# The first block's mixing in another order: plain transposes of x, squares of queries ahead of further weights, scores ahead of eight convolution taps on TensorE

## The chip, the cores and the metric

The kernel runs on one core of a Trainium2 chip. The metric is the device time of one execution in microseconds; lower is better. The core's engines are TensorE (PE, its weight loads PEld), VectorE (DVE), ScalarE (ACT), GpSimd (POOL) and SyncE (SP), which issues the loads of the large weights.

## What is computed

The input x has 256 rows (time steps) of 1024 channels. A first block mixes the rows and applies a mixture of 16 experts; a second block with another mixer and 32 experts follows. All is float32. The change lies in the first block's mixing, which in the reference reads, cut to what matters:

```python
def first_block(x, ...):
    h = rms_norm(x, attn_norm_g)
    z = h @ w_in
    a_val, a_gate, p_in, q, k, v = jnp.split(z, splits, axis=-1)
    u = a_val * sigmoid(a_gate)                       # 256 channels
    y_conv = silu(layer_norm(causal_conv31(u) + conv_b)) @ w_pw + b_pw
    y_pool = pool_mixer(p_in, pool_w, pool_scale)     # 256 channels, windows of 2, 4, 8, 16
    q = rms_norm(q.reshape(..., 4, 2, 64), q_norm_g)  # k likewise
    lam = exp(sum(lq1 * lk1)) - exp(sum(lq2 * lk2)) + lam_init
    # per head: softmax(first half) - lam * softmax(second half), times v
    y_attn = rms_norm(diff_attention(q, k, v, lam, slopes), sub_norm_g) * (1 - lam_init)
    x = x + concatenate([y_conv, y_pool, y_attn]) @ w_out
    hf = rms_norm(x, ffn_norm_g)
    return x + hier_moe(hf, ...)
```

The rms norm of x multiplies each row by a number r of its own and each channel by a gain. Since r is one number per row it may be applied before the product with `w_in` or after it.

## The kernel before, in words

x is held as two tiles of 128 rows (`xr`). TensorE needs the channels on the partitions, so x is turned into eight pieces of 128 channels by 256 rows. `rms_r` computes r, `diagonal` writes it on two diagonal matrices `rdg` (L432), and `transpose_split` multiplies x by them, so that turning and scaling are one product (`ptr`). Each piece is scaled by the gain (`colG`) on its way out of PSUM and split in a high part (`h1h`, ScalarE, L415) and a remainder (`h1l`, VectorE).

The weights are loaded in pieces: `piece` loads two halves by SP, and splits each in `hi` (ScalarE, L235) and `lo` (VectorE, L236). A product with `w_in` is then three products of TensorE: hi by h1h, lo by h1h, hi by h1l. The jobs of list `J1` hold such a piece each and run in the order in which they were added: queries, keys (`row`, result `pr`), gate, value (`ch`, result `pg`, channels on the partitions), `vv`, pool, six jobs of the modulation vector that the second block needs (`pada`: 16 products each; ScalarE's `adap`, `pac`), two of `w_out`, three more of modulation. `ahead` issues loads and splits of coming jobs; in the order that results they stand on ScalarE's and VectorE's queues among the other work.

The other work of the stage is written as generators, and `weave` takes steps of jobs and of generators alternately, at a rate (`RATE1`). The program's scheduler then orders each engine's instructions. `qk_chain` computes lambda from four small loads (`lamv`), the squares (`qsq`) and their sums (`qs`), a reciprocal root, the normalised queries and keys, and turns them (`pqt`). `conv_chain` runs the 31 taps of the convolution: the first with bias by a VectorE operation (L758), 20 by VectorE's multiply-and-add (L771, 40 instructions since there are two groups of channels), ten by ScalarE multiplications (L751) that GpSimd adds up (L768), and one addition (L777) brings the two sums together. Then follow the mean and variance by TensorE (`pmean`, `pvar`), the norm, silu (L798) and the product `ppw`. `attn_head` computes scores (`psc`), adds the distance term (L844), maxima, exponentials (ScalarE L851), the difference of the two softmaxes (L857, L858), turns it (`pat`), and multiplies it by `vv` (`po`). `attn_end` normalises the four heads' outputs and turns them (`poT`). `pool_chain` forms the windows' sums on VectorE and its product is `ppl`.

After that `ctx_prep` turns the second block's context (`ptr` of `xc`), the product with `w_out` is added to x, x is turned (`ptm`) for the router's logits (`plg`), and the router places the rows (`ppos`, `Dd`) for the first gather `pgx` of the experts.

Tiles of 8 KB come from a pool of 19 slots, PSUM from two pools of four banks (`mm` for jobs, `aux` for the rest).

Of the kernel before, what the change touches and what calls it, by code (L numbers as in the profile page):

```python
# [11 lines left out]
F32R = mybir.dt.float32r  # L12
# [10 lines left out]
KD = 8  # L23
# [7 lines left out]
ADA1 = 6  # L31
ADAR = 3
RATE1 = 1.3
RATE2 = 1.3
# [7 lines left out]
YA = 3  # L42
NPOOL = 10
TACT = 1
FILL = 2
# [77 lines left out]
def _body(es, tc, I, cst_d, msk_d, out_d, tap, stop):  # L123
# [9 lines left out]
    def U(name, shape, dt=F32):  # L133
        return gp.tile([128] + shape, dt, tag="g8", name=name)
# [520 lines left out]
    J1.row(w_in, 1792, h1f, (0, 128), lambda j, p: A.activation(t1["vv"][:, j, :], p, AF.Copy))  # L655
    J1.ch(w_in, 512, h1f, 256, lambda c, p: A.activation(t1["ppad"][:, c, 16:272], p[:, :256], AF.Copy))
    for b in range(ADA1):
# [58 lines left out]
    def qk_chain():  # L716
        lp = W("lamp", [2, 64])
        lv4 = lamv.rearrange("p (a b) d -> p a b d", b=2)
        V.tensor_tensor(lp, lv4[:, :, 0, :], lv4[:, :, 1, :], op=ALU.mult)
        ls = S("lams", [2], bufs=1)  # L720
        V.tensor_reduce(ls, lp, op=ALU.add, axis=AX.X)
        A.activation(ls, ls, AF.Exp)
        V.tensor_tensor(lam, ls[:, 0:1], ls[:, 1:2], op=ALU.subtract)
        V.tensor_scalar(lam, lam, lam_init, None, op0=ALU.add)
# [8 lines left out]
        V.tensor_tensor(qkv, qkv, qr.unsqueeze(2).to_broadcast([128, 32, 64]), op=ALU.mult)  # L733
        yield
# [14 lines left out]
    def TE(o, i, w):  # L749
        if TACT:  # L750
            A.activation(o, i, AF.Copy, scale=w)  # L751
        else:
            G.tensor_scalar(o, i, w, None, op0=ALU.mult)

    def conv_chain():

        for c in range(2):
            V.tensor_scalar(acc[:, c, :], upad[:, c, 0:256], colA[:, oCW + c:oCW + c + 1],  # L758
                            colA[:, oCB + c:oCB + c + 1], op0=ALU.mult, op1=ALU.add)

        last = 31 - NPOOL
        for j in range(last, 31):
            t = W("tap", [2, 256])
            for c in range(2):
                w = colA[:, oCW + 2 * j + c:oCW + 2 * j + c + 1]
                TE(sg1[:, c, :] if j == last else t[:, c, :], upad[:, c, j:j + 256], w)
            if j > last:
                G.tensor_tensor(sg1, sg1, t, op=ALU.add)  # L768
        for j in range(1, last):
            for c in range(2):  # L770
# [147 lines left out]
    left = weave(J1.run(ADA1), [att, chain(cvc, pool_chain())], RATE1)  # L918
    drain(both(*left))
# [1102 lines left out]
```

## Time and profile before

| | us |
|---|---|
| median of 3 runs | 1324.03 (1322.96 to 1325.92) |
| the profiled execution | 1325.26 |
| its span, first to last instruction | 1323.4 |
| TensorE busy | 1248.6 (94%) |
| VectorE busy | 662.1 (50%) |
| ScalarE busy | 424.9 (32%) |
| GpSimd busy | 38.5 (3%) |

The mean granted TensorE clock is 0.986. Sums are made against the profiled execution, which lies 1.2 us above the median. Shares of busy time over the whole span say little here, because the change lies in the first 170 us and the rest is another program; the rows of the section below are cut by stage.

### The profile page before, as it was taken

Reading aid. Unit: us, or ns where it says so; the run is one execution under the profiler, and the core shown is the slowest. Engines: PE = TensorE matmul, PEld = TensorE weight load, DVE = VectorE, ACT = ScalarE, POOL = GpSimd, SP = SyncE. Lnnn points to the kernel's source line nnn. Section 1 sums busy time; section 2 is a strip of 40 time slices with the busy share of each in tenths; the row PEclk is TensorE's granted clock in tenths of the full one; section 3 lists DMA queues with packets and bytes.
Section 4 is the critical chain, followed back from the end, with each engine's and each line's share of the span. In section 5 each row is a group of like instructions: output and inputs, shape, how many; then the busy total and the mean of one; then the engine's idle time right before and its main releaser. Section 6 shows DMA issues by size and latency. Waiting matters only on the chain. (4 is left out here: it accounts for less than half of the span.)

```text
span 1323.4 us, 19929 instructions
## 1 busy us (share of the span) xinstructions
PE 1248.6 (94%) x8098; PEld 852.8 (64%) x8098; DVE 662.1 (50%) x1444; ACT 424.9 (32%) x728; POOL 38.5 (3%) x50
## 2 busy tenths in 40 slices
PE   6988999999999999999999999899999998999895
PEld 5844566666788998898989889734435454444432
DVE  6895641125569987876574866632212222121222
ACT  5734322224334565544434443311111111010111
POOL 4110100000000000000000000100000000000000
PEclk9989899999999999999999999899999999999998
DMA  8798799983533241352525676799999999999993
GB/s 265 254 330 316 228 356 361 393 348 116 151 91 95 65 114 51 102 158 65 160 69 183 205 261 263 287 372 421 422 421 422 421 421 421 421 422 421 422 421 159
DMA packets 124355, 359.79 MB, mean 272 GB/s; under 512 B 15272, under 2 KB 64593, under 8 KB 97632
## 3 DMA queue, kind: packets, MB, share of 16 engines
q1 hardware_dynamic: 114224, 355.49, 70.6%
q10 hardware_dynamic: 9024, 2.24, 0.8%
q8 instruction: 67, 1.10, 0.3%
q0 software_dynamic: 1008, 0.70, 0.2%
q14 instruction: 32, 0.26, 0.1%
HBM read 357.35 MB, written 1.05 MB: 271 GB/s over the span
## 5 line engine op out<-in xcount | busy, mean ns | idle before, releaser
L156 PE MATMUL pg<-hT,hi 128*128 128x256 f32 (+1 forms) x1024 | 232.6, 321 | 1.5 <-DVE Qg L1363 1.5
L156 PE MATMUL pgu<-w,XT 128*64 128x256 f32 (+1 forms) x1088 | 185.9, 481 | 10.6 <-DMA w<-in_w_up_dram 10.6
L156 PEld LDWEIGHTS pg<-hT,hi 128*128 128x128 f32 x1024 | 167.2, 188 | 16.4 <-DVE Qg L1363 1.7
L236 DVE TENSOR_TENSOR lo<-w,hi 128x1024 fp32r<-128x1024 f32 x122 | 146.0, 1218 | 44.6 <-ACT hi L235 16.6
L156 PE MATMUL pdn<-w,actT 128*64 128x512 f32 x656 | 153.3, 597 | 15.6 <-ACT actT L1178 15.6
L156 PE MATMUL pg<-hT,lo 128*128 128x256 f32 (+1 forms) x512 | 162.4, 318 | 0.0
L235 ACT ACTIVATE hi<-w 128x1024 fp32r<-128x1024 f32 x122 | 125.1, 1053 | 95.5 <-PE pr L156 32.3
L156 PEld LDWEIGHTS pgu<-w,XT 128*64 128x64 f32 x1088 | 87.7, 137 | 102.2 <-issue 61.2
L156 PE MATMUL pgg<-w,XT 128*64 128x512 f32 x512 | 117.1, 596 | 1.1 <-DMA w<-in_w_gate_dram 1.1
L156 PEld LDWEIGHTS pdn<-w,actT 128*64 128x64 f32 x656 | 56.8, 136 | 94.8 <-issue 70.8
L156 PEld LDWEIGHTS pg<-hT,lo 128*128 128x128 f32 x512 | 96.2, 188 | 7.3 <-issue 0.4
L156 PE MATMUL pr<-hi,hT 128*128 128x256 f32 (+1 forms) x384 | 88.9, 321 | 0.6 <-PEq L1272 0.6
L156 PEld LDWEIGHTS pgg<-w,XT 128*64 128x64 f32 x512 | 37.0, 137 | 70.5 <-issue 63.9
L1167 DVE SCALAR_TENSOR_TENSOR act<-sgm,ws,pgu 128x512 f32<-128x512 f32 (+1 forms) x25 | 24.4, 977 | 101.7 <-PE pgu L156 101.7
L1193 DVE TENSOR_TENSOR Pg<-pdn,g 128x512 f32<-128x512 f32 x32 | 22.0, 689 | 99.4 <-PE pdn L156 99.4
L1159 DVE TENSOR_TENSOR sgm<-sgm,pgg 128x512 f32<-128x512 f32 x16 | 11.0, 688 | 116.9 <-ACT sgm L1158 116.8
L156 PEld LDWEIGHTS pr<-hi,hT 128*128 128x128 f32 x384 | 64.1, 188 | 7.2 <-issue 1.0
L1158 ACT ACTIVATE sgm<-pgg 128x512 f32<-128x512 f32 x16 | 9.6, 597 | 176.6 <-PE pgg L156 176.6
L1197 ACT ACTIVATE Ph<-Pg 128x512 fp32r<-128x512 f32 x32 | 20.2, 630 | 134.1 <-DVE Pg L1193 134.1
L156 PE MATMUL pr<-lo,hT 128*128 128x256 f32 (+1 forms) x192 | 61.8, 322 | 0.0
L156 PE MATMUL pgx<-Dd,xnh 128*128 128x256 f32 (+1 forms) x208 | 49.5, 283 | 0.1
L156 PE MATMUL pgx<-Dd,xnl 128*128 128x256 f32 (+1 forms) x208 | 49.3, 282 | 0.0
(520 smaller groups left out, 1928.4 us busy)
## 6 DMA issues: line engine op xcount, KB each, us to landing
w<-in_w_gate_dram SPq DMA_DIRECT2D x82, 1024.0 KB, 19.8
w<-in_w_up_dram SPq DMA_DIRECT2D x82, 1024.0 KB, 19.7
w<-in_w_down_dram SPq DMA_DIRECT2D x80, 1024.0 KB, 19.8
w<-in_w_in_dram SPq DMA_DIRECT2D x98, 512.0 KB, 4.6
w<-in_w_ada_dram SPq DMA_DIRECT2D x24, 1024.0 KB, 6.7
w<-in_w_out_dram SPq DMA_DIRECT2D x4, 1024.0 KB, 5.5
w<-in_w_branch_b_dram SPq DMA_DIRECT2D x8, 512.0 KB, 4.1
w<-in_w_branch_a_dram SPq DMA_DIRECT2D x8, 512.0 KB, 4.6
```

Source lines behind the costliest of these rows:

```text
L156: t2["mm"] = PE.matmul(out, lhsT, rhs, start=start, stop=stop, skip_group_check=True)
L235: t2["hi"] = A.activation(hi[:, ks], t, AF.Copy)
L236: t2["lo"] = V.tensor_tensor(lo[:, ks], t, hi[:, ks].bitcast(F32), op=ALU.subtract)
L1158: A.activation(sg, outs[0], AF.Sigmoid)
L1159: V.tensor_tensor(sg, sg, outs[0], op=ALU.mult)
L1167: V.scalar_tensor_tensor(act.rearrange("p (f c) -> p c f", f=NF), sg.rearrange("p (c f) -> p c f", f=NF), wcol, o.rearrange("p (c f) -> p ...
L1193: V.tensor_tensor(qg, q, gain[:, n, :], op=ALU.mult)
L1197: A.activation(ph, q, AF.Copy)
```

## The change

- x is turned by 16 plain transposes with the identity, before r is known. r is applied after the products: as ScalarE's scale on queries, keys and `vv` (rows on the partitions), and for gate, value and pool, where rows lie along the free dimension, by VectorE multiplications with a tile `rrow` that holds r in every partition. `rrow` comes from a product of ones with the diagonals (`prw`).
- In `qk_chain` the squares and their sums stand first, ahead of the parameters' transposes (`param_cols`) and of the splits of further weights; lambda comes after the turns of queries and keys.
- Eight taps (the last ones, 23 to 30) run on TensorE: ScalarE writes 16 diagonal matrices of 128 by 128 (`cdg`), and 16 products of 128 by 256 sum up in PSUM (`pcv`). VectorE does taps 0 to 22 (44 multiply-and-adds in place of 40). ScalarE's and GpSimd's taps go.
- Value and gate no longer share the weave with the convolution's start: `vv` comes after the query norm, and the convolution weaves with the attention and all remaining jobs. `RATE1` goes from 1.3 to 1.7, and the pool's generator waits until its input exists.

```diff
-RATE1 = 1.3
+RATE1 = 1.7
...
-NPOOL = 10
-TACT = 1
+NPE = 8
...
-               lambda j, p, qi=qi: A.activation(t1["qk"][:, 2 * qi + j, :], p, AF.Copy))
-    J1.ch(w_in, 256, h1f, 256, lambda c, p: A.activation(t1["sg1"][:, c, :], p[:, :256], AF.Sigmoid))
+               lambda j, p, qi=qi: A.activation(t1["qk"][:, 2 * qi + j, :], p, AF.Copy, scale=rx[:, j:j + 1]))
+
+    def ev_gate(c, p):
+        sg = t1["sg1"][:, c, :]
+        V.tensor_tensor(sg, p[:, :256], t1["rrow"], op=ALU.mult)
+        A.activation(sg, sg, AF.Sigmoid)
+        V.tensor_tensor(sg, sg, t1["rrow"], op=ALU.mult)
+
+    J1.ch(w_in, 256, h1f, 256, ev_gate)
...
-    J1.ch(w_in, 512, h1f, 256, lambda c, p: A.activation(t1["ppad"][:, c, 16:272], p[:, :256], AF.Copy))
+    J1.row(w_in, 1792, h1f, (0, 128), lambda j, p: A.activation(t1["vv"][:, j, :], p, AF.Copy, scale=rx[:, j:j + 1]))
+    J1.ch(w_in, 512, h1f, 256,
+          lambda c, p: t1.__setitem__("pp", V.tensor_tensor(t1["ppad"][:, c, 16:272], p[:, :256], t1["rrow"],
+                                                            op=ALU.mult)))
...
+    for kk in range(4):
+        p = ax_ps("ptr", (2, 256))
+        for i in range(2):
+            for j in range(2):
+                PE.transpose(p[:, j, 128 * i:128 * i + 128],
+                             xr[i][:, 128 * (2 * kk + j):128 * (2 * kk + j) + 128], ident)
+        for j in range(2):
+            k = 2 * kk + j
+            split_evac(h1[0][:, k, :], h1[1][:, k, :], p[:, j, :], colG[:, k:k + 1])
+        if kk == 1:
+            J1.ahead(1)
...
-    transpose_split(xr, rx, h1[0], h1[1], 0, colG, dg=rd)
+    t1["rrow"] = W("rrow", [256])
...
-    param_cols()
+    prw = ax_ps("prw", (256,))
+    for i in range(2):
+        mm(prw[:, 128 * i:128 * i + 128], ones, rd[:, i], True, True)
+    V.tensor_copy(t1["rrow"], prw)
...
+    def conv_taps():
+
+        dg = [U("cdg", [2, 8, 128]) for _ in range((NPE + 7) // 8)]
+        t1["cdg"] = lambda c, i: dg[i // 8][:, c, i % 8, :]
+        for i in range(NPE):
+            for c in range(2):
+                o = oCW + 2 * (31 - NPE + i) + c
+                A.activation(t1["cdg"](c, i), ident, AF.Copy, scale=colA[:, o:o + 1])
...
+        pcv = ax_ps("pcv", (2, 256))
+        for c in range(2):
+            for i in range(NPE):
+                j = 31 - NPE + i
+                mm(pcv[:, c, :], t1["cdg"](c, i), upad[:, c, j:j + 256], i == 0, i == NPE - 1)
...
-        if NPOOL:
-            V.tensor_tensor(acc, acc, sg1, op=ALU.add)
+        V.tensor_tensor(acc, acc, pcv, op=ALU.add)
...
-    weave(J1.run(2), [qk_chain()], 1.0)
+    qkc = qk_chain()
+    next(qkc)
+    param_cols()
+    with after(t2["qsq"]), after(t2["qkn"]):
+        J1.ahead(5)
     b1 = U("b1", [4, 512])
     vv = t1["vv"] = b1[:, 0:2, :]
     t1["osb"] = b1[:, 2:4, :]
-    cvc = conv_chain()
-    left = weave(J1.run(1), [cvc], 1.0)
     ppad = t1["ppad"] = U("ppad", [6, 288])
     V.memset(ppad[:, 0:2, 0:16], 0.0)
-    drain(J1.run(1))
+    drain(J1.run(2))
+    drain(qkc)
+    conv_taps()
     t1["ex"] = [U("ex", [2, 2, 512]) for _ in range(2)]
+    cvc = conv_chain()
     att = chain(both(*[attn_head(h) for h in range(4)]), attn_end())
-    left = weave(J1.run(ADA1), [att, chain(cvc, pool_chain())], RATE1)
+    left = weave(J1.run(2 + ADA1), [att, chain(cvc, pool_chain())], RATE1)
```

How the instructions are moved shows in the order of the engines' queues at three places. The lines of the changed kernel differ by up to some thirty from those of the kernel before.

The first place is ScalarE from the evacuation of the first keys (`qk<-pr`) to the squares (`qsq`); `cb` is the tile of constants, into which the weights of `conv_pw` and the pool are loaded as well, `lamv` holds the four vectors of lambda. Before:

```order
L651 ACTIVATE qk<-pr 128x512
L235 ACTIVATE hi<-w 128x1024
L701 DMA cb_367<-shape_consts 128x896
L706 DMA cb_367<-in_conv_pw_w_dram 128x2x256
L710 DMA cb_367<-in_pool_w_dram 64x64 x4
L235 ACTIVATE hi<-w 128x1024 x3
L651 ACTIVATE qk<-pr 128x512
L235 ACTIVATE hi<-w 128x1024
L651 ACTIVATE qk<-pr 128x512
L728 ACTIVATE qsq<-qk 128x2048
```

and in the changed kernel:

```order
L650 ACTIVATE qk<-pr,rry 128x512
L722 DMA cb_359<-shape_consts 128x896
L727 DMA cb_359<-in_conv_pw_w_dram 128x2x256
L650 ACTIVATE qk<-pr,rry 128x512
L731 DMA cb_359<-in_pool_w_dram 64x64 x4
L734 DMA lamv<-in_lambda_q_dram 128x64
L734 DMA lamv<-in_lambda_k_dram 128x64
L734 DMA lamv<-in_lambda_q_dram 128x64
L734 DMA lamv<-in_lambda_k_dram 128x64
L741 ACTIVATE qsq<-qk 128x2048
```

The loads of `lamv`, which stood far ahead among the first evacuations of x, now stand between the loads of `cb` and the squares.

The second place is VectorE around the sums of squares (`qs`); `lamp` is the product of lambda's vectors, `qry`, `qrh` and `qrt` belong to the reciprocal root, and `cv` holds the convolution's input, gate and sum. Before:

```order
L1509 TENSOR_TENSOR lbe<-colB,lbm 128x32
L730 TENSOR_REDUCE qs<-qsq 128x32
L596 TENSOR_TENSOR scp<-colC,sgc 128x8x2
L731 TENSOR_SCALAR qs<-qs 128x32
L377 TENSOR_SCALAR qry<-qs 128x32
```

and in the changed kernel:

```order
L1535 TENSOR_TENSOR lbe<-colB,lbm 128x32
L654 TENSOR_TENSOR cv<-pg,rrow 128x256
L763 TENSOR_TENSOR lamp<-lamv 128x128
L743 TENSOR_REDUCE qs<-qsq 128x32
L595 TENSOR_TENSOR scp<-colC,sgc 128x8x2
L654 TENSOR_TENSOR cv<-pg,rrow 128x256
L744 TENSOR_SCALAR qs<-qs 128x32
L656 TENSOR_TENSOR cv<-cv,rrow 128x256
L376 TENSOR_SCALAR qry<-qs 128x32
```

`lamp`, which needs all four loads, and the gate's multiplications by `rrow` have moved to the front of and between the steps of the reciprocal root.

The third place is TensorE from the convolution's last product `ppw` to the second head's output `po` and what follows it. Before:

```order
L156 MATMUL ppw<-cv,cb_367 128x256 x4
L156 MATMUL ppl<-dd,cb_367 128x256 x2
L156 MATMUL pada<-w,scp 32x512 x4
L863 MATMUL pat<-cst,ex 128x128 x3
L617 MATMUL pac<-cst,adap 128x128 x4
L156 MATMUL po<-b_569,aT 128x128 x3
L863 MATMUL pat<-cst,ex 128x128 x3
L156 MATMUL po<-b_569,aT 128x128 x3
L863 MATMUL pat<-cst,ex 128x128 x3
L156 MATMUL pr<-w,mix 128x512
```

and in the changed kernel:

```order
L155 MATMUL ppw<-cv,cb_359 128x256 x4
L155 MATMUL ppl<-dd,cb_359 128x256 x2
L884 MATMUL pat<-cst,ex 128x128 x3
L155 MATMUL pada<-w,scp 32x512
L155 MATMUL po<-b_426,aT 128x128 x3
L155 MATMUL pada<-w,scp 32x512 x3
L884 MATMUL pat<-cst,ex 128x128 x3
L616 MATMUL pac<-cst,adap 128x128 x4
L155 MATMUL po<-b_426,aT 128x128 x3
L884 MATMUL pat<-cst,ex 128x128 x3
L155 MATMUL pada<-w,scp 32x512
L155 MATMUL po<-b_426,aT 128x128 x3
```

Products of modulation (`pada`) have moved in behind `ppw` where pieces of `w_out` (`pr`) followed; ahead of `poT` six of those pieces are left where there were nine.

## Rows read from the trace of the kernel before

**Rows 1.** Busy time by stage: stretch, length, then busy us (instructions) of each engine, granted clock, DMA.

```profile
17.23:39.93 22.70, 22.70 (x100) 17.85 (x99) 15.69 (x24) 13.21 (x18) 1.75 (x4) 1.00 0.85 282
49.46:52.65 3.19, 0.00 (x0) 0.03 (x1) 3.12 (x8) 0.93 (x2) 0.00 (x0) 1.00 0.33 127
45.39:106.78 61.39, 49.14 (x316) 32.44 (x315) 59.00 (x149) 33.69 (x79) 11.39 (x9) 0.94 0.77 281
84.90:91.80 6.90, 5.08 (x21) 2.37 (x20) 6.56 (x29) 4.68 (x20) 0.00 (x0) 0.51 0.99 364
106.50:148.82 42.32, 41.08 (x166) 23.27 (x167) 18.94 (x63) 15.56 (x35) 0.00 (x0) 1.00 0.74 273
106.78:110.80 4.02, 4.02 (x23) 2.36 (x22) 3.92 (x15) 3.07 (x8) 0.00 (x0) 1.00 0.23 49
173.00:316.00 143.00, 137.70 (x996) 85.38 (x995) 37.06 (x81) 35.77 (x75) 0.00 (x0) 1.00 0.83 326
```

**Rows 2.** Timeline of TensorE, opening and context: start, us, instructions, idle time before and its releaser.

```profile
6.64 0.27 PE L212 MATMUL pcol<-cst,stage 8*128 8x8 f32 x1 [6.64 <-DMA stage<-in_attn_norm_g_dram]
10.95 6.55 PE L156 MATMUL ptr<-rdg,xr 128*128 128x128 f32 x32 [4.04 <-DVE rdg L432]
17.26 0.48 PE L156 MATMUL pr<-hi,h1h 128*128 128x512 f32 x1
...
130.48 3.73 PE L156 MATMUL ptr<-rdg,xc 128*128 128x128 f32 x32
```

**Rows 3.** Timeline of ScalarE up to the squares.

```profile
9.49 1.06 ACT L235 ACTIVATE hi<-w 128x1024 fp32r<-128x1024 f32 x1 [3.12 <-DMA w<-in_w_in_dram]
...
28.49 0.58 ACT L651 ACTIVATE qk<-pr 128x512 f32<-128x512 f32 x1
...
32.88 0.45 ACTq L706 DMA_DIRECT2D cb<-in_conv_pw_w_dram  x1
...
43.44 1.92 ACT L728 ACTIVATE qsq<-qk 128x2048 f32<-128x2048 f32 x1
```

**Rows 4.** Loads: of tile lamv, from issue to landing; of conv_pw, KB and us to landing.

```profile
DMA to landing us min/median/max: 4.1/4.4/6.2
...
cb<-in_conv_pw_w_dram ACTq DMA_DIRECT2D x1, 256.0 KB, 6.4
```

**Rows 5.** Timeline of VectorE from the squares to the router, and of GpSimd.

```profile
45.39 2.29 DVE L730 TENSOR_REDUCE qs<-qsq 128x32 f32<-128x2048 f32 x1 [0.24 <-ACT qsq L728]
...
55.81 2.35 DVE L236 TENSOR_TENSOR lo<-w,hi 128x1024 fp32r<-128x1024 f32 x2
58.08 0.42 DVE L654 TENSOR_TENSOR cv<-pg,cv 128x256 f32<-128x256 f32 x1
...
59.13 14.88 DVE L771 SCALAR_TENSOR_TENSOR cv<-cv,colA 128x256 f32<-128x256 f32 x16
...
73.97 4.80 DVE L771 SCALAR_TENSOR_TENSOR cv<-cv,colA 128x256 f32<-128x256 f32 x12
...
168.63 0.76 DVE L1089 TENSOR_TENSOR Dd<-cst,pe 128x256 fp32r<-128x256 f32 x2
...
59.72 12.02 POOL L768 TENSOR_TENSOR cv<-cv,tap 128x512 f32<-128x512 f32 x9 [39.93 <-ACT tap L751]
```

**Rows 6.** Timeline of TensorE from the queries' turns to the router.

```profile
52.65 1.94 PE L744 MATMUL pqt<-cst,qk 128*128 128x128 f32 x16 [3.19 <-DVE qk L733]
...
84.59 2.11 PE L156 MATMUL psc<-qkT 64*128 64x128 f32 x8 [4.07 <-DVE ex L844]
...
106.50 1.99 PE L156 MATMUL ppw<-cv,cb 128*128 128x256 f32 x8 [1.05 <-DVE cv L798]
...
111.07 0.66 PE L617 MATMUL pac<-cst,adap 128*128 128x128 f32 x4 [0.24 <-ACT adap L614]
...
124.43 0.74 PE L893 MATMUL poT<-cst,b 128*128 128x128 f32 x5 [0.37 <-DVE b L884]
...
168.08 1.07 PE L156 MATMUL pada<-w,scp 128*32 128x512 f32 x8
```

More of the change, by code (lines that the diff above doesn't have):

```diff
@@ L650, in _body @@
         J1.row(w_in, 768 + 512 * qi, h1f, (0, 128),
-               lambda j, p, qi=qi: A.activation(t1["qk"][:, 2 * qi + j, :], p, AF.Copy))
-    J1.ch(w_in, 256, h1f, 256, lambda c, p: A.activation(t1["sg1"][:, c, :], p[:, :256], AF.Sigmoid))
+               lambda j, p, qi=qi: A.activation(t1["qk"][:, 2 * qi + j, :], p, AF.Copy, scale=rx[:, j:j + 1]))
[5 more added lines that the diff above has]
+    J1.ch(w_in, 256, h1f, 256, ev_gate)
     J1.ch(w_in, 0, h1f, 256,
           lambda c, p: V.tensor_tensor(t1["upad"][:, c, 30:286], p[:, :256], t1["sg1"][:, c, :], op=ALU.mult))
-    J1.row(w_in, 1792, h1f, (0, 128), lambda j, p: A.activation(t1["vv"][:, j, :], p, AF.Copy))
-    J1.ch(w_in, 512, h1f, 256, lambda c, p: A.activation(t1["ppad"][:, c, 16:272], p[:, :256], AF.Copy))
+    J1.row(w_in, 1792, h1f, (0, 128), lambda j, p: A.activation(t1["vv"][:, j, :], p, AF.Copy, scale=rx[:, j:j + 1]))
+    J1.ch(w_in, 512, h1f, 256,
+          lambda c, p: t1.__setitem__("pp", V.tensor_tensor(t1["ppad"][:, c, 16:272], p[:, :256], t1["rrow"],
+                                                            op=ALU.mult)))
     for b in range(ADA1):
@@ L664, in _body @@
         ada_job(J1, b, True)
+    h1 += [U("h1h", [KD, 256], F32R), U("h1l", [KD, 256], F32R)]
+    for kk in range(4):
[9 more added lines that the diff above has]
+            J1.ahead(1)
     rx = rms_r(xr)
-    h1 += [U("h1h", [KD, 256], F32R), U("h1l", [KD, 256], F32R)]
     rd = diagonal(rx)
-    with after(t2["rdg"]):
-        J1.ahead(1)
-    transpose_split(xr, rx, h1[0], h1[1], 0, colG, dg=rd)
+    t1["rrow"] = W("rrow", [256])
     A.dma_start(cst[:, C_J:C_N], cst_d[:, C_J:C_N])
@@ L716, in qk_chain @@
     def qk_chain():
[L717 to L724, printed above, removed]
         qsq = U("qsq", [32, 64])
@@ L727, in qk_chain @@
         qkv = qk.rearrange("p a (g d) -> p (a g) d", d=64)
-        A.activation(qsq, qkv, AF.Square)
+        t2["qsq"] = A.activation(qsq, qkv, AF.Square)
         qs = S("qs", [32], bufs=1)
@@ L732, in qk_chain @@
         qr = rsqrt(qs, [32], "qr")
-        V.tensor_tensor(qkv, qkv, qr.unsqueeze(2).to_broadcast([128, 32, 64]), op=ALU.mult)
+        t2["qkn"] = V.tensor_tensor(qkv, qkv, qr.unsqueeze(2).to_broadcast([128, 32, 64]), op=ALU.mult)
         yield
@@ L747, in qk_chain @@
             yield
[L749 to L753, printed above, removed]
-    def conv_chain():
+        lp = W("lamp", [2, 64])
+        lv4 = lamv.rearrange("p (a b) d -> p a b d", b=2)
+        V.tensor_tensor(lp, lv4[:, :, 0, :], lv4[:, :, 1, :], op=ALU.mult)
+        ls = S("lams", [2], bufs=1)
+        V.tensor_reduce(ls, lp, op=ALU.add, axis=AX.X)
+        A.activation(ls, ls, AF.Exp)
+        V.tensor_tensor(lam, ls[:, 0:1], ls[:, 1:2], op=ALU.subtract)
+        V.tensor_scalar(lam, lam, lam_init, None, op0=ALU.add)
+    def conv_taps():
[5 more added lines that the diff above has]
+                A.activation(t1["cdg"](c, i), ident, AF.Copy, scale=colA[:, o:o + 1])
+    def conv_chain():
+        pcv = ax_ps("pcv", (2, 256))
[3 more added lines that the diff above has]
+                mm(pcv[:, c, :], t1["cdg"](c, i), upad[:, c, j:j + 256], i == 0, i == NPE - 1)
         for c in range(2):
@@ L759, in conv_chain @@
                             colA[:, oCB + c:oCB + c + 1], op0=ALU.mult, op1=ALU.add)
[L761 to L769, printed above, removed]
+        for j in range(1, 31 - NPE):
             for c in range(2):
@@ L806, in pool_chain @@
     def pool_chain():
+        while "pp" not in t1:
+            yield
         ppad = t1["ppad"]
```

## The prediction

> **What bounds the kernel now.** I read the busy time by stage first, then the timeline of each engine across the stages that the change touches. The first mixture of experts, 173 to 316 us, keeps TensorE busy for 137.70 of 143.00 us [rows 1]; from there on the instructions of all engines follow in the same order before and after, so I let a shift at the router's end pass 1:1 to the end. Ahead of it lie four stages. From 17.23 to 39.93 us TensorE is never idle, with the 96 products of queries and keys (0.23 us each) [rows 1]; the first of them waited for the turned x, which waited 4.04 us for VectorE's diagonal `rdg` [rows 2]. From the sums of squares at 45.39 to the last product of the convolution's norm at 106.78 VectorE is busy 59.00 of 61.39 us while TensorE has 49.14 [rows 1]: VectorE sets that stage. From 106.50 to 148.82 TensorE does 41.08 of 42.32 us [rows 1] and sets the stage. Last comes the router. The sum is therefore one of four terms: when the sums of squares start, how long VectorE's stage is, how long TensorE's tail is, and the router.
>
> **A. The opening.** `rdg` and the wait for it go. The plain turns need x and the norm's weights alone and can begin behind `pcol` at 6.64 [rows 2] instead of 10.95; they take at most the 6.55 us of the old ones, interleaved with their evacuations. The first product then waits for a weight: its first high part runs from 9.49 to 10.55, because its load landed only then [rows 3], and the low part takes another 1.2 (half of 2.35) [rows 5]. So the products begin at 10.6 to 11.8 instead of 17.26. What runs there may run slowly: the 16 old turns took 6.55 us, the same 16 of another tensor 3.73 later [rows 2], so I read the first as done at the lower level (1.2 GHz), and the upper one as reached by 17.26, from where a product takes 0.23. Five microseconds of products at half speed would give back 2.5. SP issues the weights in the same order, but the second to fourth of them now wait for other small loads; that too is in the ends. The products end at 34.0 to 36.4; I take 35.2, **4.7 earlier**.
>
> **B. The squares, and a new wait ahead of them.** Nominally the squares (1.92 us on ScalarE [rows 3], then the reduction on VectorE) now follow the last evacuation at once. But in the new order the four little loads `lamv` stand on ScalarE between the loads of `cb` and the squares, and on VectorE `lamp`, which needs all four, stands in front of the reduction. The program gives each load of ScalarE and SP one of a few common semaphores in turn, and its waits show that a `lamv` cannot be issued until `cb` has landed, and a later one not until `conv_pw` has. Before, `lamv` was loaded during the opening and nobody waited. The time: the last 12 products are 2.8 us, so the third evacuation starts at 35.2 - 2.8 = 32.4, takes 0.58 [rows 3], `cb` and then `conv_pw` follow, 0.45 for an issue [rows 3], so that `conv_pw` goes out by 33.7 and lands 6.4 us later [rows 4], at 40.1. That `lamv` is issued then and lands after 4.1 to 6.2 us [rows 4], and `lamp` runs before the reduction, which so starts at 44.5 to 46.6. I take 45.3, against 45.39 [rows 5]: **-0.1**, the opening's gain is swallowed. With the ends of A and shorter or longer landings it is 42.1 to 47.6, so -3.3 to +2.2. The Trainium skill (DMA: Bandwidth & Descriptors, Anatomy of one DMA) puts a load's fixed part at about 2 us, and so a 32 KB load at hardly more; by that the reduction would start near 42.5 and this term would be -2.9. The rows of this same load say 4.1 at least, and I follow them.
>
> **C. VectorE's stage, 61.39 us before.** Removed: while GpSimd added its nine taps (12.02 us), VectorE's 16 taps took 14.88, 0.93 each; with GpSimd silent 12 took 4.80, 0.40 each [rows 5]. No GpSimd adds are left, so 16 x 0.53 = -8.5. Added: four more taps, +1.6 (8 taps of 31 move to TensorE, but 10 had been on ScalarE and GpSimd); five multiplications by `rrow`, from PSUM, 0.42 each as the value product is [rows 5], +2.0; the parts of lambda, formerly ahead of the stage, +0.5; four more low parts of weights, since all of `vv` and the pool's pieces now follow the query norm, 4 x 1.15 = +4.6. At the end 1.5 heads' softmax and the pool's last products lay behind the norm: VectorE was busy 3.92 of 4.02 us there [rows 1]. One head's share and these products, some 2.3, now stand in front, +2.3. That makes -8.5 + 1.6 + 2.0 + 0.5 + 4.6 + 2.3 = +2.5. VectorE was idle for 2.4 us of the stage; since taps now stand ready at more of its waits, I take all of that to go: **+0.1**. With half of it left, or some of the small operations falling into ScalarE's and TensorE's waits, the ends are -2 and +2. TensorE's 16 products of `pcv` are priced by `ppw`, 8 records in 1.99 us, 0.50 for each of its four products [rows 6]: 16 x 0.46 to 0.50 = 7.4 to 8. TensorE had 12 us to spare, and 8 fewer modulation products (2.1) stand in the stage, so I cost them at nothing here. That cover fails if the clock falls. ScalarE's 18 taps go and 16 diagonals of a quarter of the area come: nothing.
>
> **D. TensorE's tail.** Between `ppw` and `poT` there were one half of a modulation job and two pieces of `w_out` among the attention outputs; now there are three halves. The total of `w_out` is unchanged, so 8 products of `pada` more, 16 records at 8 in 1.07 [rows 6], +2.1; one more `pac`, 0.66 [rows 6], +0.6. Of `w_out` only six products, not nine, are left as cover when the attention norm runs, and each `po` now waits for ScalarE, which also has two more `adap` evacuations in that chain; before, `poT` waited 0.37 [rows 6]. I take +1.7 for the waits, some 0.4 at each of four heads, 0.2 to 2.3 as ends: **+4.4**, +2.9 to +5.
>
> **E. The router.** `ppos` was followed by 8 records of `pada`, 1.07 us, while VectorE made `Dd` [rows 5, 6]. Now `pada` stands first and nothing covers `Dd`: **+1.0**, 0 to 1.
>
> Sum: -0.1 + 0.1 + 4.4 + 1.0 = +5.4. B and E have their longer ends towards less (-3.3 against +2.2, and 0), so I forecast 0.8 under it, **+4.6**. The profiled execution took 1325.26 us (span 1323.4), so 1329.9 for one like it; it lay 1.2 above the median of 1324.03, so the forecast for a median is **1328.6 us**. A measurement of this kernel tells 0.2%, 2.6 us, from no change.
>
> **The rivals.**
> *The opening's gain arrives and the clock holds (faster).* Place: the reduction `qs`. If `lamv` lands in time and it starts at 42.1, -3.3; if C is at its lower end, -2; and if TensorE, with `pcv` and the scores spread out, has no idle time like the 4.07 us ahead of `psc` [rows 6], after which the granted clock was 0.51 for 6.9 us, with 5.08 us of work [rows 1], half of that work comes back, -2.5. Against it stand +3.5 of tail and router near their lower ends: -4.3, a median near 1319.7. It decides when the reduction starts before about 42 us. For it: the rows of GpSimd's contention are plain, 8.5 us. Against: ScalarE's order.
>
> *A short landing (no change).* `lamv` lands within 2 to 3 us of its issue, B is -2.9, the rest as taken: +2.6, or less with it, medians of 1322 to 1326.6. It decides at a start of 42 to 43. This is what the Trainium skill's fixed part of a load (DMA: Bandwidth & Descriptors, Anatomy of one DMA) would make of the case. Against it stand the 4.1 us of the fastest `lamv` [rows 4], for it that the queue may be emptier than it was in the opening.
>
> *A second fall of the clock (slower still).* In front of `pqt` TensorE now waits for the whole chain of squares, with 6 us more of VectorE work (`rrow`, taps, lambda) strewn into it. 3.19 us of idle time there did not lower the clock [rows 1, 6], 4.07 did. I expect 6 to 9 us idle ahead of `pqt`, and a fall there is within C's ends; another 3.7 ahead of `ppw`, where there was 1.05 [rows 6], would put the first 6.9 us of the tail at half speed: +3.4, a median of 1332. With the load of `lamv` late too, 1334. The Trainium skill (TensorE: Matmul & The Clock Gate, HAM oscillation — how this bites in real kernels) says that a TensorE which pauses between bursts falls back to its lower level and pays for the rise again each time; this speaks against the change, and by it this case would be the likelier one. The rows show one such fall in this stage, not one at each wait.
>
> That the change doesn't do what it says: `pcv` could hold the stage, were TensorE full; 49.14 + 8 - 2 of 61.39 says no, and I give it no share of its own.
>
> **How the numbers follow.** My forecast, slower by 3 to 7 us, 0.45; the second fall, 0.13; both make slower, 0.58. The short landing, 0.22, is all of no change. The faster rival gets 0.20, since C's largest term is the surest row here. The range runs from 1319.5, the middle of the faster case, to 1334.0, the end of the second fall; about 0.1 lies below and some 0.07 above. The likeliest case's own range is 1326.7 to 1331.
>
> **What would show it.** Right: first `pr` near 11; `lamv` issued near 34 to 40 and `qs` preceded by a wait for it; taps at 0.40 throughout; `ppw` within 2 us of 106.5; waits for `aT` at every `po`; `pgx` waiting for `Dd`. Wrong: `qs` before 42 with no wait for a load; `ppw` before 103; a tail from `ppw` to `ptm` no longer than before.

## The result and the profile after

The changed kernel takes **1339.34 us** (median of 4 runs, 1337.86 to 1339.91), the kernel before, timed beside it, 1324.97: the ratio is 1.0102, 95% interval 1.0084 to 1.012. It is slower, as forecast, but by 14.4 us where 4.6 were forecast, and outside the range. The profiled execution took 1339.91 us, its span is 1338.1 against 1323.4: **14.7 us** have to be found.

The busy time by stage, with columns as in [rows 1]. First two stretches of the kernel before, from `ppw` to `ptm` and from there to `pgx`:

```profile
106.50:148.65 42.15, 40.91 (x165) 23.11 (x165) 18.94 (x63) 15.56 (x35) 0.00 (x0) 1.00 0.74 274
148.65:169.20 20.55, 19.05 (x123) 11.18 (x122) 15.38 (x69) 8.47 (x14) 6.10 (x4) 0.75 0.87 274
```

and the stretches of the changed kernel:

```profile
46.23:109.17 62.94, 51.29 (x310) 35.72 (x309) 59.39 (x175) 31.97 (x78) 0.00 (x0) 0.94 0.65 228
108.90:115.50 6.60, 6.60 (x17) 4.73 (x17) 1.48 (x6) 2.33 (x5) 0.00 (x0) 0.53 1.05 386
108.90:159.88 50.98, 49.89 (x184) 26.66 (x185) 16.43 (x55) 15.03 (x33) 0.00 (x0) 0.94 0.84 319
159.88:182.88 23.00, 16.84 (x124) 10.45 (x122) 16.62 (x69) 9.79 (x15) 6.08 (x4) 0.85 0.85 280
183.00:187.00 4.00, 4.00 (x22) 4.00 (x23) 2.27 (x11) 0.95 (x2) 0.00 (x0) 0.57 0.96 383
```

The account, by the starts of `qs`, `ppw`, `ptm` and `pgx`:

| stage | before | after | more | forecast |
|---|---|---|---|---|
| start to `qs` | 45.39 | 46.23 | +0.8 | -0.1 |
| `qs` to `ppw` | 61.11 | 62.67 | +1.6 | +0.1 |
| `ppw` to `ptm` | 42.15 | 50.98 | +8.8 | +4.4 |
| `ptm` to `pgx` | 20.55 | 23.00 | +2.4 | +1.0 |
| `pgx` to the end | 1154.2 | 1155.2 | +1.0 | 0 |

With the 0.8 that the forecast took off its own sum, these differences make up the missing 10.1 us. Most of it lies in TensorE's tail. TensorE is busy 1262.4 us after and 1248.6 before, 13.8 more, with nearly as many records (8118 against 8098): most of that is the same work at a higher price, as the lines below show.

TensorE in the changed kernel, turns of the queries and tail:

```profile
56.32 3.65 PE L757 MATMUL pqt<-cst,qk 128*128 128x128 f32 x16 [5.29 <-DVE qk L746]
...
108.90 3.78 PE L155 MATMUL ppw<-cv,cb 128*128 128x256 f32 x8 [3.86 <-DVE cv L817]
112.47 1.91 PE L155 MATMUL ppl<-dd,cb 128*128 128x256 f32 x4
114.18 0.85 PE L884 MATMUL pat<-cst,ex 128*128 128x128 f32 x3
114.96 1.11 PE L155 MATMUL pada<-w,scp 128*32 128x512 f32 x2
116.00 0.94 PE L155 MATMUL po<-b,aT 128*128 128x128 f32 x6
116.86 1.06 PE L155 MATMUL pada<-w,scp 128*32 128x512 f32 x6
...
120.28 1.04 PE L155 MATMUL pada<-w,scp 128*32 128x512 f32 x2
121.25 0.94 PE L155 MATMUL po<-b,aT 128*128 128x128 f32 x6
122.12 1.06 PE L155 MATMUL pada<-w,scp 128*32 128x512 f32 x6
...
127.25 0.66 PE L616 MATMUL pac<-cst,adap 128*128 128x128 f32 x4 [0.77 <-ACT adap L613]
127.75 5.32 PE L155 MATMUL pr<-w,mix 128*128 128x512 f32 x12
133.09 1.06 PE L914 MATMUL poT<-cst,b 128*128 128x128 f32 x8
```

Two things stand there that the sum did not have. `pqt` takes 3.65 us for 16 records where it took 1.94 [rows 6], and `ppw` 3.78 where it took 1.99: both run at the lower clock level, 1.2 GHz (granted 0.50 from 56.3 to 59.7, and 0.53 from 108.9 to 115.5, nearly all of it at that level), behind waits of 5.29 and 3.86 us. And a piece of `pada` costs about 1.0 us whether it has one product (2 records) or three (6 records); before, four in a row cost 1.07 [rows 6]. The products are 32 columns wide; four that stand together run side by side. The scheduler put `po` into each of the three sets of the tail, so that three sets cost six times 1.0.

The router, TensorE and then ScalarE of the changed kernel:

```profile
171.53 1.12 PE L616 MATMUL pac<-cst,adap 128*128 128x128 f32 x4 [4.38 <-ACT adap L613]
172.44 1.06 PE L624 MATMUL paq<-cst,adap 128*128 128x128 f32 x4
173.43 3.46 PE L155 MATMUL pada<-w,scp 128*32 128x512 f32 x16
...
182.88 0.36 PE L155 MATMUL pgx<-Dd,xnh 128*128 128x256 f32 x1 [1.05 <-DVE Dd L1115]
```

```profile
169.49 1.28 ACT L1016 ACT_TABLE_LOAD   x1
170.79 0.21 ACT L1016 ACTIVATE gx<-gx 128x8 f32<-128x8 f32 x1
```

`pgx` waits 1.05 us for `Dd`, as forecast. The load of the exponential's table at 169.49 is new. Before, the scores still needed exponentials behind the convolution's sigmoid, so the table was loaded there already:

```profile
105.80 1.28 ACT L851 ACT_TABLE_LOAD   x1
```

After, the sigmoid comes last (106.26), the router's first exponential has to load the table in its own chain, and TensorE idles 4.38 us.

The opening, TensorE at the second weight, then ScalarE and VectorE of the changed kernel:

```profile
15.72 0.80 PE L155 MATMUL pr<-hi,h1h 128*128 128x512 f32 x1 [0.65 <-ACT hi L234]
```

```profile
14.61 1.06 ACT L234 ACTIVATE hi<-w 128x1024 fp32r<-128x1024 f32 x1 [2.63 <-DMA w<-in_w_in_dram]
...
38.42 2.46 ACTq L731 DMA_DIRECT2D cb<-in_pool_w_dram  x4
40.92 0.60 ACTq L734 DMA_DIRECT2D lamv<-in_lambda_q_dram  x1
...
43.02 1.91 ACT L741 ACTIVATE qsq<-qk 128x2048 f32<-128x2048 f32 x1 [3.92 <-DMA cb<-in_pool_w_dram]
```

```profile
46.02 0.29 DVE L763 TENSOR_TENSOR lamp<-lamv 128x128 f32<-128x128 f32 x1 [3.59 <-DMA lamv<-in_lambda_k_dram]
46.23 2.28 DVE L743 TENSOR_REDUCE qs<-qsq 128x32 f32<-128x2048 f32 x1
```

The first product ran at 11.31 us, as forecast, and the products ended at 38.2, not at 35.2. The second weight landed only at 14.6, but TensorE waited just 0.65 us for it. The larger loss is speed: the first 16 products, from 11.31 to 19.65, start some 0.43 us apart, later ones 0.23. (The row of that stretch gives a granted clock of 1.00 all the same; the durations show the slowness.) The squares `qsq` waited 3.92 us on ScalarE behind the issue of `cb` and `lamv`. `lamp` stands in front of `qs` and waits 3.59 us for `lamv`, as forecast.

### The profile page after: what moved, and what is told of

It is laid out like the page before. It is cut to its first block, busy times and chain, and to the rows that moved or that the text cites. A ratio compares the mean times of both kernels' runs of the same rounds, so it can differ in the third digit from the quotient of the medians.

```text
span 1338.1 us, 19949 instructions
## 1 busy us (share of the span) xinstructions
PE 1262.4 (94%) x8118; PEld 862.9 (64%) x8118; DVE 656.5 (49%) x1455; ACT 421.4 (31%) x722; POOL 27.1 (2%) x41
## 3 DMA queue, kind: packets, MB, share of 16 engines
HBM read 357.35 MB, written 1.05 MB: 268 GB/s over the span
## 5 line engine op out<-in xcount | busy, mean ns | idle before, releaser
L155 PE MATMUL pgx<-Dd,xnh 128*128 128x256 f32 (+1 forms) x208 | 52.2, 292 | 1.9 <-DVE Dd L1115 1.9
L155 PE MATMUL pgx<-Dd,xnl 128*128 128x256 f32 (+1 forms) x208 | 52.1, 291 | 0.0
```

The lines of the kernel that those rows point to most:

```text
L155: t2["mm"] = PE.matmul(out, lhsT, rhs, start=start, stop=stop, skip_group_check=True)
```

## The experiments

My theory after reading the two traces: the tail is longer because sets of `pada` are broken (2.9 us) and because TensorE enters it at half clock (about 2.8: `ppw` 3.57 us to the next start against 1.83, `ppl` 1.71 against 0.95, `pat` 0.3 more), on top of the two more sets and one `pac` that were forecast (2.7); the router is longer by the table's load. Rivals: the tail is long because of the waits of `po` (the forecast's own term), or the late `lamv` is what costs. A second question is which part of the change sends work into the tail. Every kernel below was timed together with the kernel before; its ratio and 95% interval are against that.

**Whole sets again: the changed kernel with a lower rate, at which the order keeps the sets together.**

```diff
-RATE1 = 1.7
+RATE1 = 1.5
```

> The changed kernel with RATE1 1.5 in place of 1.7. In the order that results, the modulation's products stand between ppw and poT as whole sets of four (four sets, three pac, nine pieces of w_out ahead of poT), where the changed kernel has two of its three sets broken up as one, po, three. Theory of the broken sets (four products of a set use a quarter of the array each and run side by side, so one alone costs as much as four): each set here takes 1.0 us and not 2.0; from ppw to ptm 50.98 - 2.9 + 1.6 for one set and one pac more = about 49.7. Theory of the record (only the number of products counts, waits for the rest): 50.98 + 1.6 = 52.6. [...]

Measured: 1334.91 us (ratio 1.0062, 1.0043 to 1.0081). The timeline of TensorE and the stretch from `ppw` to `ptm`:

```profile
114.06 1.06 PE L155 MATMUL pada<-w,scp 128*32 128x512 f32 x8
...
117.11 1.06 PE L155 MATMUL pada<-w,scp 128*32 128x512 f32 x8
```

```profile
108.03:156.00 47.97, 46.54 (x196) 25.54 (x197) 19.04 (x62) 15.19 (x34) 0.00 (x0) 0.97 0.89 341
```

The tail fell by 3.0 us although it holds one set more (four whole ones against three; the expectation counts two of the three as broken, the lines of the changed kernel show all three). The count closes: three sets more than before at 1.0, two `pac` more at 0.6 and `ppw` at half clock, 1.5, make 5.7 of the 5.82 by which it exceeds the kernel before. Broken sets are confirmed, though not all of the 3.0 is theirs: four whole sets in place of six pieces save 2.0, one `pac` more costs 0.6, and some 1.3 comes from half speed, which ended sooner here (1.5 in place of 2.8). The waits of `po` are not needed.

**The table loaded where ScalarE is idle.**

```diff
+        A.activation(S("etl", [1], bufs=1), sq[:, 1, 0:1], AF.Exp)
         for co in range(2):
```

> The changed kernel with one exponential of a single number per partition added behind the convolution's sigmoid; its result is not used. It brings the exponential's table back while ScalarE is idle. Theory of the table (the router's first exponential now pays 1.28 us of table load in the chain that the modulation's pac waits for): from ptm to pgx 23.00 becomes 21.7, and since in the order that results the last half of modulation stands behind ppos again, 20.7; the total falls by 2.3, and by 1.3 more if TensorE's wait ahead of pac gets too short for the clock to fall. Rival (the router is late because of the clock or of VectorE's chain): 22.5 or more from ptm to pgx, total within 1 us of the changed kernel.

Measured: 1335.32 us (1.0074, 1.0051 to 1.0098). ScalarE and TensorE in the router:

```profile
167.99 0.20 ACT L1017 ACTIVATE gx<-gx 128x8 f32<-128x8 f32 x1
```

```profile
168.69 0.66 PE L616 MATMUL pac<-cst,adap 128*128 128x128 f32 x4 [1.34 <-ACT adap L613]
...
176.80 1.06 PE L155 MATMUL pada<-w,scp 128*32 128x512 f32 x8
177.92 0.35 PE L155 MATMUL pgx<-Dd,xnh 128*128 128x256 f32 x1
```

The load now stands at 108.45 in ScalarE's idle time. The router takes 19.34 us, 3.65 less than in the changed kernel and 1.2 less than before. The starts divide the 3.65. From `ptm` to the first `pac` it is 10.11 in place of 11.65: 1.5, the load that is gone from ScalarE's chain. (The wait of `pac` fell by more, from 4.38 to 1.34, because the `pada` in front of it ran at half speed here.) From the first to the second `pac` it is 4.83 in place of 6.09: 1.3, products at full speed behind the shorter wait. From there to `pgx` it is 4.40 in place of 5.26: 0.9, because the scheduler put a set of `pada` behind `ppos` again, which hides `Dd`. The granted clock is 0.91 over the stage against 0.85 and, before, 0.75, and 1.00 in the first four microseconds of the gather. The tail, in the same order as in the changed kernel, is 1.4 us shorter (49.54), mostly because half speed ended sooner: its price differs between executions.

**The clock held through the convolution's norm:** eight unused products while VectorE makes the norm.

```diff
         rs = rsqrt(mv_, [256], "ln")
+        pf = ax_ps("fil")
+        for i in range(8):
+            mm(pf[:, :256], ones, rs, True, True)
```

> The changed kernel with eight products of 128 by 256 added, whose result is not used; they stand on TensorE in the idle time ahead of ppw. Theory of the clock: TensorE is not idle there, ppw takes 1.99 us for its 8 records and not 3.78, and the first 7 us of the tail run at full clock: -3.3; one more set of modulation products is broken up in this order, +1.0, so from ppw to ptm 48.7 in place of 50.98 and a total 2 us lower. Rival (ppw and what follows are slow for another reason, the loads of w_out for example): ppw still takes 3.7 us and the total rises by about 1.

Measured: 1337.98 us (1.0089, 1.0058 to 1.0119).

```profile
104.46 3.72 PE L155 MATMUL fil<-lny,cst 128*128 128x256 f32 x16 [0.62 <-DVE lny L382]
...
109.08 1.99 PE L155 MATMUL ppw<-cv,cb 128*128 128x256 f32 x8
```

The clock is 1.00 from 108.9 to 115.5, `ppw` takes 1.99 us again, and `ppw` to `poT` fell from 24.19 to 22.33 although one piece of `pada` more stands there (1.0): the half clock had cost about 2.8. Over the whole kernel the span is 1.7 us shorter (1336.4); the medians' intervals can't tell that from nothing.

**The loads of `lamv` early, as in the kernel before.**

```diff
     J1.ahead(2)
+    lamv = W("lamv", [4, 64])
+    for j, nm in enumerate(("lambda_q1", "lambda_k1", "lambda_q2", "lambda_k2")):
+        A.dma_start(lamv[:, j, :], I[nm][0].partition_broadcast(128))
...
-    lamv = W("lamv", [4, 64])
-    for j, nm in enumerate(("lambda_q1", "lambda_k1", "lambda_q2", "lambda_k2")):
-        A.dma_start(lamv[:, j, :], I[nm][0].partition_broadcast(128))
```

> The changed kernel with the four loads of lamv issued early, ahead of the first evacuations of queries. Theory of the wait (step B): the squares follow the last evacuation at once, the sums of squares start at 41.3 in place of 46.23, and if VectorE sets the stage, ppw starts 4 to 5 us earlier than 108.9 and the total falls by 4 to 5. Rival (the stage is set by the weights of vv, whose loads wait for VectorE's splits, or by something else): sums of squares at 41.3 all the same, but ppw at 107 or later and the total within 2 us.

Measured: 1338.2 us (1.0083, 1.0058 to 1.0109).

```profile
42.64:107.93 65.29, 55.69 (x340) 38.89 (x338) 60.12 (x175) 33.12 (x78) 0.00 (x0) 0.94 0.67 234
```

`qs` starts at 42.64, 3.6 us earlier, but `ppw` only 1.0: the stage between grew from 62.67 to 65.29. VectorE's waits there name TensorE (2.7 us for the scores) and ScalarE (0.9 for the gate's sigmoid). The wait for `lamv` is real and not what bounds.

**The parts one at a time, on the kernel before.** First the eight taps on TensorE alone:

```diff
-NPOOL = 10
-TACT = 1
+NPE = 8
...
+        pcv = ax_ps("pcv", (2, 256))
+        for c in range(2):
+            for i in range(NPE):
+                j = 31 - NPE + i
+                mm(pcv[:, c, :], t1["cdg"](c, i), upad[:, c, j:j + 256], i == 0, i == NPE - 1)
...
+    conv_taps()
     cvc = conv_chain()
```

> The kernel before with one part of the change alone: eight taps on TensorE, the other 23 on VectorE, none on ScalarE and GpSimd. Step C's ledger: 16 taps lose GpSimd's contention (-8.5), four taps more (+1.6), so VectorE's stage gets 6.9 shorter; if VectorE sets it, ppw starts near 100 in place of 106.5 and the total falls by 5 to 7. Rival (TensorE sets the stage once it has pcv's 7.4 us more): ppw 104 or later and the total within 2 us of before.

Measured: 1331.58 us (1.0045, 1.0032 to 1.0058). VectorE's costliest group, before and here:

```profile
L771 DVE SCALAR_TENSOR_TENSOR cv<-cv,colA 128x256 f32<-128x256 f32 x40 | 25.4, 687 | 0.4
```

```profile
L769 DVE SCALAR_TENSOR_TENSOR cv<-cv,colA 128x256 f32<-128x256 f32 x44 | 18.6, 475 | 0.3
```

The stage, then TensorE, then VectorE behind its last tap:

```profile
45.08:108.84 63.76, 55.04 (x354) 38.86 (x352) 54.64 (x163) 29.96 (x76) 0.00 (x0) 0.96 0.76 271
```

```profile
60.84 7.07 PE L155 MATMUL pcv<-cv,cdg 128*128 128x256 f32 x32
...
108.84 3.78 PE L155 MATMUL ppw<-cv,cb 128*128 128x256 f32 x8 [3.71 <-DVE cv L795]
```

```profile
82.28 0.69 DVE L810 TENSOR_TENSOR ppad<-ppad 128x512 f32<-128x512 f32 x1 [6.22 <-ACT ppad L655]
```

The taps gained what the forecast said: 44 at 475 ns, where 40 took 687 on average. VectorE has 4.1 us less to do (54.64 against 58.72), and the stage is still 2.7 longer. Its taps are done at 76.1 (82.05 before), but then it waits 6.22 us for the pool's input: the products of the pool stand behind the 7 us of `pcv` on TensorE, which has no idle time from 54.95 on until 93. Then `ppw` waits 3.71 us and runs at half clock. This part alone costs 5.7 us by the medians; of the 7.4 us by which the spans differ, 2.7 lie in the stage, 2.7 in the tail, 1.4 in the router and 1.0 behind it.

The plain turns and the late r alone (the diff of the change without its taps, order and rate):

```diff
-    transpose_split(xr, rx, h1[0], h1[1], 0, colG, dg=rd)
+    t1["rrow"] = W("rrow", [256])
...
+    prw = ax_ps("prw", (256,))
+    for i in range(2):
+        mm(prw[:, 128 * i:128 * i + 128], ones, rd[:, i], True, True)
+    V.tensor_copy(t1["rrow"], prw)
```

> The kernel before with another part alone: plain turns of x, and r applied after the products. As in the changed kernel, lamv stands behind the loads of cb in the order that results. Theory of the record (the opening's gain is lost in the wait for lamv, and VectorE has 2 us more): sums of squares at 45 to 47, ppw 1 to 3 us later than 106.5, total +1 to +3. Rival (the opening's gain is kept where the rest of the order is the old one): sums of squares at 42, total -1 to -3.

Measured: 1329.18 us (1.0025, 1.0013 to 1.0038). VectorE:

```profile
45.61 4.63 DVE L236 TENSOR_TENSOR lo<-w,hi 128x1024 fp32r<-128x1024 f32 x4 [3.12 <-ACT hi L235]
50.16 0.42 DVE L657 TENSOR_TENSOR cv<-cv,rrow 128x256 f32<-128x256 f32 x1
50.49 0.28 DVE L742 TENSOR_TENSOR lamp<-lamv 128x128 f32<-128x128 f32 x1
50.70 2.28 DVE L753 TENSOR_REDUCE qs<-qsq 128x32 f32<-128x2048 f32 x1
```

A miss for both theories: `qs` starts at 50.70, later than either had it, because in this order four splits of weights stand on VectorE ahead of `lamp` and `qs`, and their `hi` on ScalarE behind the late issue of `lamv`. The profiled execution is the slowest of its ten runs; the median is 3.3 us above the kernel before. The gain of the opening does not arrive.

The rate alone (`RATE1` from 1.3 to 1.7 in the kernel before):

> The kernel before with RATE1 1.7 alone. In the order that results one more set of modulation products, whole, stands in the tail, and the scores come before more of the others. Theory: +1.6 for the set and its pac in the tail, and the wait ahead of ppw longer than 1.05; total +1 to +4. Rival (the rate moves nothing that bounds): within 1 us.

Measured: 1327.88 us (1.0016, 1.0004 to 1.0029).

```profile
105.09 3.67 PE L156 MATMUL ppw<-cv,cb 128*128 128x256 f32 x8 [2.01 <-DVE cv L798]
```

`ppw` starts 1.4 us earlier and runs at half clock; `ppw` to `ptm` takes 46.72, 4.6 more, by the half clock, by a wait of 1.94 for `adap` and by a set of `pada` that moved from the stage into the tail. The rate alone costs 2.0 us.

The counterpart, the changed kernel with the taps of the kernel before (ScalarE and GpSimd, no `pcv`):

```diff
-NPE = 8
+NPOOL = 10
+TACT = 1
...
-        V.tensor_tensor(acc, acc, pcv, op=ALU.add)
+        if NPOOL:
+            V.tensor_tensor(acc, acc, sg1, op=ALU.add)
```

> The changed kernel with the convolution of the kernel before: ten taps on ScalarE and GpSimd, 21 on VectorE, no pcv. If VectorE sets the stage from squares to ppw, the contention with GpSimd costs up to 8.5 less 1.6: ppw 5 to 7 later than 108.9. Rival (TensorE's 7.4 us of pcv cost as much as they save): ppw within 2 us of 108.9 or earlier.

Measured: 1343.3 us (1.0134, 1.0117 to 1.015). VectorE's groups from `qs` to `ppw`:

```profile
L793 DVE SCALAR_TENSOR_TENSOR cv<-cv,colA 128x256 f32<-128x256 f32 x40 | 20.7, 567 | 0.0
L236 DVE TENSOR_TENSOR lo<-w,hi 128x1024 fp32r<-128x1024 f32 x6 | 12.0, 2041 | 0.0
```

So the same part that costs 5.7 us alone seems to save some 3 in the changed kernel (17.4 us above the kernel before here, 14.4 with it; the two intervals touch). There GpSimd's adds (from 55.23 on) fall on the splits of weights, which take 2041 ns each where they take 1221 with GpSimd silent.

**The repairs together.** The table and the rate of 1.5:

> The changed kernel with two of the repairs: the exponential that brings the table back, and RATE1 1.5. If the two causes are separate their gains add: 1339.3 - 4.0 - 4.4 = 1331, with 19.3 us from ptm to pgx and 48.0 from ppw to ptm. Rival (one gain takes the other's place): 1334 or more.

Measured: 1332.63 us (1.0062, 1.0044 to 1.008). By the medians that is 6.7 us below the changed kernel, where the two gains add up to 8.4; by the ratio it is no better than the lower rate alone (1.0062). The trace has both gains (48.67 from `ppw` to `ptm`, 19.78 in the router), but `qs` starts at 48.91, 2.7 later than in the changed kernel, because `lamv` is issued later still. So this settles neither view. Then with the fill and the early `lamv` as well:

> The changed kernel with all four repairs: table, RATE1 1.5, products that keep TensorE busy ahead of ppw (result not used), lamv early. The sum of the single gains is -4.0 - 4.4 - 1.4 - 1.1: 1328.5; ppw x8 in 1.99 us, ppw to ptm 46 to 47. What is left over before is then the two or three modulation sets that pcv has pushed into the tail (1.6 each with its pac). Rival: a fifth cause, total 1331 or more.

Measured: 1331.71 us (1.006, 1.0041 to 1.0079), on the rival's side.

```profile
106.14:154.53 48.39, 46.08 (x203) 24.63 (x203) 18.82 (x62) 16.65 (x36) 0.00 (x0) 1.00 0.84 323
```

`ppw` starts at 106.14, earlier than before, the clock is 1.00 and the router is short, and the tail still takes 6.2 us more than before. That is now a count: 19 products of `pada` in five pieces against four in one (+4.0), two more `pac` (+1.2), and waits of 2.3 us against 1.25 (+1.0). And without the fill, with the rate of 1.3:

> The changed kernel with RATE1 1.3, the table and lamv repairs and no filling products. The order has seven of eight products of a job behind ppw and two more halves: more work in the tail, whole sets. Theory (work in the tail counts, and the clock falls ahead of ppw): 1330 to 1333, ppw x8 over 3 us. Rival (the rate decides little): as the one with RATE1 1.5, 1331.

Measured: 1329.93 us (1.0048, 1.0032 to 1.0064), the lowest median of the repaired kernels; their intervals overlap.

**Does the clock's fall ahead of the scores cost the kernel before anything?** Nine unused products there:

```diff
+        if hd == 1:
+            pf = mm_ps("fil")
+            with after(t2["mm"]):
+                for i in range(9):
+                    PE.matmul(pf[:, :256], ones, upad[:, 0, 0:256], start=True, stop=True, skip_group_check=True)
```

> The kernel before with nine products of 128 by 256 added, whose result is not used, where TensorE is idle for 4.07 us ahead of the third head's scores. Theory of the clock: no idle time of 4 us there, the granted clock stays at 1.0 from 84.9 to 91.8, and pmean starts earlier than 91.43; if TensorE or what waits for it bounds that stretch, the total falls by 1 to 2.5, a version better than both. Rival (VectorE bounds it, so TensorE's clock costs nothing there): clock 1.0, but ppw at 106 or later and the total within 1 us.

Measured: 1324.88 us against 1324.53 (1.0005, 0.9991 to 1.0019).

```profile
82.11 0.70 PE L156 MATMUL psc<-qkT 64*128 64x256 f32 x2
...
88.19 1.11 PE L617 MATMUL pac<-cst,adap 128*128 128x128 f32 x4 [3.47 <-ACT adap L614]
```

The wait ahead of `psc` went and another of 3.47 us came 4 us later, with half clock behind it for a part (granted 0.68 from 84.9 to 91.8, 0.51 before); `ppw` did not move forward (107.11). No version beat the kernel before.

## Why the prediction was right in its sign and wrong in its size

**A, the opening: wrong by 3 us, and without weight.** First product near 11: right. The end at 35.2 was wrong, 38.2. The term that failed is "Five microseconds of products at half speed would give back 2.5": the first 16 products took 8.3 us, where 0.23 each would be 3.7, so slowness and the 0.65 us for the second weight gave back 4.6. That is 2.1 of the 3 us; the rest I have not traced.

**B, the squares: mechanism right.** The gain of the opening is swallowed by `lamv`; `qs` at 46.23, forecast 45.3. It came out near by two errors of opposite sign: the loads went out later (40.92 instead of 40.1) behind later products, and landed faster. They landed 2.9 to 3.7 us after issue, below the 4.1 to 6.2 of [rows 4]. The Trainium skill (DMA: Bandwidth & Descriptors, Anatomy of one DMA) gives about 2 us as the fixed part of a load that GpSimd issues. These four went out on ScalarE's queue, and none landed that fast. That B came so close was luck, not knowledge of the load. The early `lamv` then showed that this term prices little: 3.6 us at `qs` became 1.0 at `ppw`.

**C, VectorE's stage: size within its ends, the price of `pcv` wrong where it was tried alone.** +1.6 where I had +0.1, ends -2 and +2. VectorE's own work came as forecast: -8.5 + 1.6 is -6.9 for the taps, and alone they went from 25.4 to 18.6 us. The step that failed there is "TensorE had 12 us to spare ... so I cost them at nothing here". The run with the taps alone shows it: VectorE lost work, and the stage grew by 2.7, because VectorE then waited 6.22 us for a product that stood behind `pcv`. TensorE's idle time in the changed kernel lies in waits of the chain itself (5.29 ahead of `pqt`, 3.86 ahead of `ppw`, 2.5 elsewhere, of 11.7); work that is put elsewhere doesn't fill it, it delays what stands behind it. That `pcv` could hold the stage I had named and given no share; tried alone, it does.

**D, the tail: the main failure, +8.8 for +4.4.** Two of its terms came true: two more sets and one `pac`, 2.7 us. The failed step is the price, "16 records at 8 in 1.07". That row is four products side by side, and the third extract of the order, ahead of the prediction, already showed them as one and three with `po` between; six pieces at 1.0 make 2.9 more. The Trainium skill (TensorE: Matmul & The Clock Gate, Part 3: Packing small matmuls — row/col tiling) says that products of 32 columns in different column tiles run at the same time, 2.38 times as fast for three. The measurement here differs: one and three cost nearly the same, 1.04 and 1.06, which is 2.9 times as fast. The term for waits of `po`, +1.7, was wrong: TensorE's waits from `ppw` to `poT` add up to 1.1 us, and to 1.25 before, and no `po` waits for `aT`. In place of +1.7 of waits stand the 2.9 of broken sets and the 2.8 of half speed.

**The second fall of the clock happened.** I gave it 0.13 and it is the rival that came true, at +2.8 where I had +3.4, ahead of `ppw` by 3.86 us where I had written 3.7; and ahead of `pqt`, 5.29. The Trainium skill's rule (TensorE: Matmul & The Clock Gate, HAM oscillation — how this bites in real kernels), by which this case was the likelier one, agrees with the trace: the three longest waits here (5.29, 3.86, 4.38) are each followed by half speed. I had argued "one such fall in this stage, not one at each wait" from a kernel that had only one wait of that length. The size is not fixed: in the runs half speed behind `ppw` cost between 1.4 and 2.8 us.

**E, the router.** `Dd` +1.05: right. The reload of the exponential's table, 1.28 us on the critical chain, was missed: the order of sigmoid and exponentials on ScalarE showed it and I read ScalarE's queue only up to the squares. At the gather the clock was 0.57 in its first 4 us, and its 32 records took 5.46 us where they took 3.81, which covers the +1.0 behind `pgx`: the assumption that a shift passes 1:1 from there was off by that. This goes with the uncovered `Dd`: in all six kernels whose `pgx` waits 1.05 us for it (the changed one, and the runs with rate 1.5, fill, early `lamv`, taps alone and old taps) those 4 us are at 0.57 to 0.64; in the others, with `pada` behind `ppos`, they are at 1.00, but for one (0.53, all repairs with rate 1.3).

Of the signs that I had named, `ppw` came 2.4 us after the forecast 106.5, the waits of `po` did not come, and `lamv` went out at 40.92, behind the 34 to 40 that I had given.

What stays open: the three parts alone (5.7, 3.3 and 2.0) add up to 11.0 of 14.4 us, but they don't simply add, as the taps show, and the new order of queries, value and convolution was not tried by itself. With table, rate and early `lamv` mended, 5 to 7 us remain. In the run with all repairs most of the tail's excess is products of `pada` that stood in the stage before. It isn't `pcv` that sends them there: between `ppw` and `poT` stand four of them before, three with the taps alone, eight with the turns alone or the rate alone, twelve in the changed kernel and sixteen in it with the old taps. That points to the rate and the new order; which of the two does how much is not shown.

## What to carry to other kernels

Price an instruction in the company in which the new order leaves it: four narrow products that run side by side cost as much as one alone, so a scheduler that slips something between them doubles them. Idle time of an engine is cover only where work can be put into that very wait; otherwise the added work delays what stands behind it on that engine, and whoever waits for that (6.2 us of VectorE in the run with the taps alone). When exponentials and sigmoids change their order, look which table is left for the next user, and when a wait in front of a busy stretch grows, look at the clock behind it.

## What the runs showed of the hardware that was not expected

- Products of 128 by 32 by 512: one costs 1.04 us, three 1.06, four 1.07, when they stand together in the four column groups.
- The clock fell behind waits of 5.29, 4.38, 3.86 and 3.71 us, and not behind 3.19 [rows 6]; but with the rate alone `ppw` ran at half speed after a wait of only 2.01. It ran so behind waits of 2.59 (`pqt`, taps alone) and 2.73 (`ppw`, turns alone) as well. The length of the last wait alone does not decide.
- GpSimd's adds slow VectorE's splits of weights (two tensor inputs) from 1221 to 2041 ns each; in the kernel before they slowed the taps instead.
- The four loads of `lamv` took 2.9 to 3.7 us on the same queue on which they took 4.1 to 6.2 before. Issued early again in the changed kernel they took 4.6 to 5.6.
